# A mixture of experts as one stream of weight pieces in a hand-written order, and leading tiles in five pools

## The chip, the core and the metric

The kernel runs on one core of a Trainium2 chip. TensorE (PE) multiplies; its weight loads, which bring the stationary operand, are listed apart as PEld. VectorE is DVE, ScalarE is ACT, GpSimd is POOL; SP issues most of the DMAs. SBUF and PSUM are the on-chip memories, HBM holds weights and inputs. The metric is the device time of one execution in microseconds (us); the median of three runs is given.

## What is computed

A transformer of three layers on 256 tokens of width 1024: sliding-window attention and a dense feed-forward block, block-sparse attention and a mixture of experts, then a block of a linear and an axial attention, attention over a memory, and a second feed-forward block. All inputs are float32. The change is in the mixture of experts:

```python
def _swiglu(x, w_gate, w_up, w_down):
    return (jax.nn.silu(x @ w_gate) * (x @ w_up)) @ w_down

def _moe(x, router, w_gate, w_up, w_down):
    ...
    vals, ids = lax.top_k(logits, TOP_K)            # TOP_K = 2
    w = jax.nn.softmax(vals, axis=-1)
    gate = jnp.sum(jax.nn.one_hot(ids, N_EXPERTS, dtype=jnp.float32) * w[..., None], axis=1)
    for e in range(N_EXPERTS):                      # 8 experts, D_FF = 3584
        out = out + gate[:, e:e + 1] * _swiglu(xt, w_gate[e], w_up[e], w_down[e])
```

## The kernel before

**A product.** To keep float32 accuracy with the fast matmul, each operand is split into a high and a low part, and a product is three matmuls: high by high, high by low, low by high (lines 274, 275, 276). In `gemm` the activations are stationary, 128 by 128, and the weights move, 512 columns at a time.

**A piece of weights** is 2 by 128 rows by 512 columns, 512 KB. `fetch` (line 210) has SP issue its DMA into one of `NRAW = 9` raw buffers; `split_w` casts it on ACT into `wh` (line 256) and subtracts on DVE for `wl` (line 257), into one of `NSPL = 5` split buffers. A raw buffer is free again when DVE has read it, a split buffer when PE has used it. Where `fine` is set, the split is made in halves (lines 253, 254).

**The experts' loop** (`moe`) goes over pairs of experts. A one-hot matrix `oh` of the pair gathers its tokens by matmul (`bring`, line 1102) into `xg`, high and low, in four steps of two slices; each step is called when the first gate product reaches its slices. Then for each expert, seven times: a gate product of four pieces, Silu on ACT into `sil` (line 1162), an up product of four pieces, the multiplication on DVE (line 1170), four transposes of the result (line 186) and their split into `h` by ACT and DVE (lines 189, 190). After these come two down products of 14 pieces each; each is scaled into `yh` and `yl` (lines 1179, 1180), scattered back to the token order by four matmuls (lines 1084, 1085) and added (line 1087). The last 16 slices of the last expert's second down product are loaded early into four parked tiles (`park`). Five pieces are split and nine fetched ahead of the loop.

**The order.** All these are written one after the other, and the tile scheduler decides at build time how they follow each other on each engine; on the chip each engine runs its list in order, and each instruction waits for what it needs. PSUM has four `mm` buffers, two `tr` and two `at`.

**Pools.** Tiles stand one behind the other in their pool, so a small tile at its head moves those behind it. The pool "moe" opens with such a tile of 48 floats per partition. The pools "heads" (`oh`, `ol`, twice), "ffn" (`hh`, `hl`, used by both feed-forward blocks), "mixm" (`mh`, `ml`, `ah`, `al`) and "mem" (another `oh`, `ol`, on the right side) have none; these tiles are the stationary operands of the products behind them.

Of the kernel before, what the change touches and what calls it, by code (L numbers as in the profile page):

```python
# [8 lines left out]
F32 = mybir.dt.float32  # L9
# [7 lines left out]
P = 128  # L17
D = 1024
# [6 lines left out]
def f(ap):  # L25
    return ap.bitcast(F32)
# [72 lines left out]
class Net:  # L99
# [417 lines left out]
    def swa(self):  # L517
        nc, A, tc = self.nc, self.A, self.tc
        self.fine = True
        with ExitStack() as c0:  # L520
            po = c0.enter_context(self.pool("heads", 1))
            oh = po.tile([P, 8, T], F32R, name="oh")
            ol = po.tile([P, 8, T], F32R, name="ol")
            c = c0.enter_context(ExitStack())
# [88 lines left out]
    def ffn_body(self, Wg, g0, Wu, u0, dff, Wd, emit, scale=None, beside=lambda p: None):  # L613
# [3 lines left out]
        chunks = [(j, min(512, dff - j)) for j in range(0, dff, 512)]  # L617
        with ExitStack() as c:
            p = c.enter_context(self.pool("ffn", 1))
            hh = p.tile([P, nkf, T], F32R, name="hh")  # L620
            hl = p.tile([P, nkf, T], F32R, name="hl")
            sil = {}

            def emit_g(i, c0, n, ps, tts=(0, 1)):
                for tt in tts:
                    s = p.tile([P, 512], F32, tag="sil", name="sil", bufs=3)
                    nc.scalar.activation(s[:, :n], ps[tt][:, :n], AF.Silu, scale=scale[tt] if scale else 1.0)
                    sil[tt] = s

            j, n = chunks[0]  # L630
            self.gemm(self.xs, Wg, KD, [(g0 + j, n)], emit_g, apart=(0,))

            def emit_u(i, c0, n, ps, tts=(0, 1)):
                for tt in tts:
                    s = sil[tt][:, :n]
                    nc.vector.tensor_mul(s, s, ps[tt][:, :n])
                    self.transpose_split(s, n // P, hh[:, :n // P, tt * P:(tt + 1) * P], hl[:, :n // P, tt * P:(tt + 1) * P])

            self.gemm(self.xs, Wu, KD, [(u0 + j, n)], emit_u)
            R = None  # L640
            if scale:

                ones, R = (p.tile([P, w], F32, name=x) for x, w in (("ones", P), ("R", T)))
                nc.gpsimd.memset(ones, 1.0)
                tp = self.tr.tile([P, T], F32, tag="tr", name="tr")
                for tt in range(2):
                    nc.gpsimd.tensor_scalar_mul(R[:, tt * P:(tt + 1) * P], self.idn, scale[tt])
                    nc.tensor.matmul(tp[:, tt * P:(tt + 1) * P], ones, R[:, tt * P:(tt + 1) * P], start=True, stop=True)
                nc.scalar.copy(R, tp)

            for j, n in chunks[1:]:
                s = p.tile([P, 4, T], F32, tag="silT", name="sil", bufs=2)
                k0 = j // P

                def gate(b, ps):
                    x = s[:, 2 * b:2 * b + 2]
                    if R is not None:
                        nc.vector.tensor_mul(x, ps, R.unsqueeze(1).to_broadcast([P, 2, T]))
                    nc.scalar.activation(x, x if R is not None else ps, AF.Silu)

                def up(b, ps):
                    x, k = s[:, 2 * b:2 * b + 2], k0 + 2 * b
                    nc.vector.tensor_mul(x, x, ps)
                    nc.scalar.copy(hh[:, k:k + 2], x)
                    nc.vector.tensor_sub(hl[:, k:k + 2], x, f(hh[:, k:k + 2]))

                self.gemm_f(Wg, g0 + j, n, gate)
                self.gemm_f(Wu, u0 + j, n, up)
                if j == 512:
                    beside(p)  # L670
            self.gain = None
            self.gemm(lambda k, tt: (hh[:, k, tt * P:(tt + 1) * P], hl[:, k, tt * P:(tt + 1) * P]), Wd, nkf,
                      [(0, 512), (512, 512)], emit, apart=(1,))
# [29 lines left out]
    def nsa(self):  # L703
        nc, A, tc = self.nc, self.A, self.tc
        self.fine = True
        with ExitStack() as c0:
            po = c0.enter_context(self.pool("heads", 1))
            c = c0.enter_context(ExitStack())
            p = c.enter_context(self.pool("nsa", 1))
            qT = tuple(p.tile([P, 8, T], F32R, name=f"q{n}") for n in "hl")  # L710
# [272 lines left out]
    def moe(self):  # L983
# [5 lines left out]
        with ExitStack() as c0:  # L989
# [103 lines left out]
            def gather(oh):  # L1093

                xg = [p.tile([P, KD, 2, P], F32R, tag=f"xg{n}", name="xg") for n in "hl"]

                def bring(k0):
                    for X, x in zip((Xh, Xl), xg):
                        ps = self.mm.tile([P, 2, 2, P], F32, tag="mm", name="mm")
                        for k in range(2):  # L1100
                            for tt in range(2):
                                nc.tensor.matmul(ps[:, k].rearrange("p a s -> p (a s)"), X[tt][:, (k0 + k) * P:(k0 + k + 1) * P],  # L1102
                                                 oh[:, tt].rearrange("p a s -> p (a s)"), start=tt == 0, stop=tt == 1)
                        if X is Xl:
                            nc.scalar.copy(x[:, k0:k0 + 2], ps)  # L1105
                        else:
                            nc.vector.tensor_copy(x[:, k0:k0 + 2], ps)

                there = set()

                def xs(i, k):
                    if k not in there:
                        there.update((k, k + 1))
                        bring(k)
                    return xg[0][:, k, i], xg[1][:, k, i]

                return xs


            for n in range(NRAW + NSPL):  # L1120
# [22 lines left out]
                    nc.vector.scalar_tensor_tensor(y, ps if h else y, mu, out["g"][:, cs], op0=OP.subtract, op1=OP.mult)  # L1143
                    nc.vector.scalar_tensor_tensor(x, y, rs, out["b"][:, cs], op0=OP.mult, op1=OP.add)

            for e0 in range(0, NE, 2):
                oh, back = onehots((e0, e0 + 1), 0)
                brought = gather(oh)
                if e0 == 0:

                    last = [self.xp.tile([P, 4, 512], F32, tag="xh", name="parked"), *(p.tile([P, 4, 512], F32, name=f"parked{n}") for n in range(3))]
                    for n, t in enumerate(last):
                        self.park(Wd[NE - 1], (NF - 16 + n * 4) * P, 512, t)
                for i in range(2):
                    e = e0 + i
                    hs = {}
                    xs = lambda k, tt: brought(i, k)
                    st = {}

                    def emit_g(_, c0, n, ps, tts=(0, 1)):  # L1160
                        st["s"] = p2.tile([P, 512], F32, tag="sil", name="sil")
                        nc.scalar.activation(st["s"], ps[0], AF.Silu)

                    for j in range(F // 512):
                        self.gemm(xs, Wg[e], KD, [(j * 512, 512)], emit_g, tts=(0,))
                        if i == 0 and j == 0:
                            oT, gs = back()

                        def emit_u(_, c0, n, ps, tts=(0, 1)):
                            nc.vector.tensor_mul(st["s"], st["s"], ps[0])  # L1170
                            hs[j] = [p.tile([P, 4, P], F32R, tag=f"h{n}", name="h", bufs=7) for n in "hl"]
                            self.transpose_split(st["s"], 4, hs[j][0], hs[j][1])

                        self.gemm(xs, Wu[e], KD, [(j * 512, 512)], emit_u, tts=(0,))

                    def emit_d(_, c0, n, ps, tts=(0, 1)):
                        yh = p.tile([P, 512], F32R, tag="yh", name="yh")
                        yl = p.tile([P, 512], F32R, tag="yl", name="yl")
                        nc.scalar.mul(yh, ps[0], gs[:, i:i + 1])
                        nc.vector.scalar_tensor_tensor(yl, ps[0], gs[:, i:i + 1], f(yh), op0=OP.mult, op1=OP.subtract)  # L1180
                        scatter(yh, yl, oT, i, c0, e == NE - 1)

                    if e == NE - 1:
                        out["g"] = self.bcast(A["ln_gain"][1, 1], D, "gb", pool=p, tag="xgh")
                        out["b"] = self.bcast(A["ln_bias"][1, 1], D, "bb", pool=p, tag="xgl")
                    for c0 in (0, 512):
                        self.fine = e == NE - 1 and c0 > 0
                        self.gemm(lambda k, tt: (hs[k // 4][0][:, k % 4], hs[k // 4][1][:, k % 4]), Wd[e], NF,
                                  [(c0, 512)], emit_d, tts=(0,))

        self.routes.close()

# [134 lines left out]
    def mixer(self):  # L1327
# [3 lines left out]
        with ExitStack() as c0:  # L1331
# [46 lines left out]
            with self.tc.high_priority(offset=-1000):  # L1378
                self.memory_kv()
            pm = c0.enter_context(self.pool("mixm", 1))  # L1380
            mh = pm.tile([P, KD, T], F32R, name="mh")
            ml = pm.tile([P, KD, T], F32R, name="ml")
            ah = pm.tile([P, 8, T], F32R, name="ah")
# [461 lines left out]
    def memory(self):  # L1845
# [3 lines left out]
        with ExitStack() as c0:  # L1849
# [3 lines left out]
            qT = p.tile([P, 8, T], F32, name="qT")  # L1853
            oh = po.tile([P, 8, T], F32R, tag="oh", name="oh")
            ol = po.tile([P, 8, T], F32R, tag="ol", name="ol")
            ms = lambda k, tt: (oh[:, k, tt * P:(tt + 1) * P], ol[:, k, tt * P:(tt + 1) * P])
            self.new_xT()
            with self.pool("pre", 1) as px:
# [212 lines left out]
```

## Time and profile before

| | |
|---|---|
| median of three runs | 2371.4 us (2369.98 to 2378.29) |
| the profiled execution | 2368.1 us; its span 2366.3 us |
| busy, share of the span | PE 96%, PEld 81%, DVE 75%, ACT 61%, POOL 3% |
| mean granted clock of TensorE | 0.977 |
| HBM read | 536 MB, 228 GB/s over the span |

Busy shares are means over stages that differ. A matmul is listed from its start to the modelled end of its pipeline, so two that follow each other overlap; the rate is read from start to start. "Idle before" is the time in which the engine stood still ahead of an instruction, with what ended it.

### The profile page before, as it was taken

To read this page: it belongs to the slowest core of one execution; us is meant where nothing else is said; L and a number is where in the kernel's file an instruction comes from. 1 tells how busy PE (TensorE), PEld (TensorE's weight loads), DVE (VectorE), ACT (ScalarE), POOL (GpSimd) and SP (SyncE) were. 2 spreads that over 40 slices of the span, in tenths; PEclk is the share of its full clock that TensorE was granted. 3 is DMA by queue.
4 is the path that set the end of the run, shared out by engine and by line. 5 is a ranking of instruction groups with operands and counts; after the bars stand their busy time and mean duration, and the time that the engine had idled before them with its cause. 6 is when DMAs were issued, how large, how long until landed. Compare 5 with 4: busy or idle time off the path is not lost.

```text
span 2366.3 us, 35741 instructions
## 1 busy us (share of the span) xinstructions
PE 2261.2 (96%) x12969; PEld 1923.0 (81%) x12969; DVE 1778.9 (75%) x2849; ACT 1440.7 (61%) x2386; POOL 66.1 (3%) x78
## 2 busy tenths in 40 slices
PE   8999998999899999999999999996898999989998
PEld 6699977887787787778777877775898888988997
DVE  7765559766788988889888888887857765666664
ACT  5664436665677767777777777774553554455553
POOL 0000000000000000000000000001110110000000
PEclk9999999999899999999999999998998999999999
DMA  8366555434899999999999999994333213543761
GB/s 242 98 198 192 187 160 175 148 107 145 289 364 350 350 350 345 357 352 343 346 365 349 358 334 357 355 323 132 108 90 99 74 54 110 170 143 137 260 200 46
DMA packets 319711, 541.96 MB, mean 229 GB/s; under 512 B 21839, under 2 KB 95015, under 8 KB 319271
## 3 DMA queue, kind: packets, MB, share of 16 engines
q1 hardware_dynamic: 309680, 528.93, 66.6%
q10 hardware_dynamic: 9847, 10.67, 1.5%
q8 instruction: 104, 1.70, 0.3%
q14 instruction: 80, 0.66, 0.1%
HBM read 536.38 MB, written 3.15 MB: 228 GB/s over the span
## 4 chain that ended last, share of the span: by engine, by line
PE 65%; DVE 4%; issue 3%; ACT 1%; POOL 1%; DMA 0%; DVEq 0%; POOLq 0%; ACTq 0%
PE mm L275 15%; PE mm L276 15%; PE mm L274 15%; PE tr L186 2%; PE mm L688 1%; PE mm L318 1%; PE mm L689 1%; PE mm L687 1%; PE mm L319 1%; PE mm L317 1%; PE tr L1701 1%; DVE wl L254 1%; PE at L1712 1%; PE at L1715 1%; PE mm L1102 1%
## 5 line engine op out<-in xcount | busy, mean ns | idle before, releaser
L257 DVE TENSOR_TENSOR wl<-w,wh 128x1024 fp32r<-128x1024 f32 x755 | 884.4, 1219 | 171.9 <-ACT wh L256 166.9
L256 ACT CAST wh<-w 128x1024 fp32r<-128x1024 f32 x755 | 753.9, 1050 | 179.3 <-PE mm L276 114.2
L275 PE MATMUL mm<-wl,xg 128*128 128x512 f32 x896 | 364.8, 407 | 0.6
L276 PE MATMUL mm<-wh,xg 128*128 128x512 f32 x896 | 351.4, 392 | 0.0
L274 PE MATMUL mm<-wh,xg 128*128 128x512 f32 x896 | 349.7, 392 | 0.0
L253 ACT CAST wh<-w 128x512 fp32r<-128x512 f32 (+1 forms) x378 | 216.3, 616 | 135.5 <-PE mm L276 59.6
L254 DVE TENSOR_TENSOR wl<-w,wh 128x512 fp32r<-128x512 f32 (+1 forms) x378 | 247.1, 682 | 52.0 <-ACT wh L253 51.5
L275 PEld LDWEIGHTS mm<-wl,xg 128*128 128x128 f32 x896 | 168.4, 188 | 65.8 <-DVE wl L257 35.7
L274 PEld LDWEIGHTS mm<-wh,xg 128*128 128x128 f32 x896 | 168.2, 188 | 36.0
L276 PEld LDWEIGHTS mm<-wh,xg 128*128 128x128 f32 x896 | 168.8, 188 | 30.9 <-ACT xg L1105 1.4
L687 PE MATMUL mm<-xh,wh 128*128 128x256 f32 x672 | 187.4, 279 | 0.0
L689 PE MATMUL mm<-xl,wh 128*128 128x256 f32 x672 | 187.3, 279 | 0.0
L688 PE MATMUL mm<-xh,wl 128*128 128x256 f32 x672 | 187.3, 279 | 0.0
L275 PE MATMUL mm<-wl,h 128*128 128x512 f32 x448 | 177.1, 395 | 1.7 <-DVE wl L257 1.7
L276 PE MATMUL mm<-wh,h 128*128 128x512 f32 x448 | 174.6, 390 | 0.0
L274 PE MATMUL mm<-wh,h 128*128 128x512 f32 x448 | 174.5, 390 | 0.0
L687 PEld LDWEIGHTS mm<-xh,wh 128*128 128x128 f32 x672 | 127.4, 190 | 0.0
L688 PEld LDWEIGHTS mm<-xh,wl 128*128 128x128 f32 x672 | 126.3, 188 | 0.0
L689 PEld LDWEIGHTS mm<-xl,wh 128*128 128x128 f32 x672 | 126.2, 188 | 0.0
L275 PEld LDWEIGHTS mm<-wl,h 128*128 128x128 f32 x448 | 84.1, 188 | 22.8 <-DVE wl L257 6.1
L274 PEld LDWEIGHTS mm<-wh,h 128*128 128x128 f32 x448 | 84.1, 188 | 18.0 <-ACT wh L256 0.2
L276 PEld LDWEIGHTS mm<-wh,h 128*128 128x128 f32 x448 | 84.2, 188 | 16.6 <-issue 0.2
(615 smaller groups left out, 4466.7 us busy)
## 6 DMA issues: line engine op xcount, KB each, us to landing
w<-in_moe_w_gate_dram SPq DMA_DIRECT2D x224, 512.0 KB, 5.6
w<-in_moe_w_up_dram SPq DMA_DIRECT2D x224, 512.0 KB, 5.5
w<-in_moe_w_down_dram SPq DMA_DIRECT2D x216, 512.0 KB, 5.9
w<-in_w_in_dram SPq DMA_DIRECT2D x60, 512.0 KB, 3.8
w<-in_w_ffn_in_dram SPq DMA_DIRECT2D x40, 512.0 KB, 9.8
w<-in_ffn_w_gate_dram SPq DMA_DIRECT2D x28, 512.0 KB, 4.5
w<-in_ffn_w_up_dram SPq DMA_DIRECT2D x28, 512.0 KB, 4.4
w<-in_ffn_w_down_dram SPq DMA_DIRECT2D x28, 512.0 KB, 3.6
```

Source lines behind the costliest of these rows:

```text
L186: nc.tensor.transpose(ps[:, k, :], src[:, (k0 + k) * P:(k0 + k + 1) * P], self.idn)
L253: nc.scalar.copy(wh[:, ks, :n], w[:, ks, :n])
L254: nc.vector.tensor_sub(wl[:, ks, :n], w[:, ks, :n], f(wh[:, ks, :n]))
L256: nc.scalar.copy(wh[:, :nk, :n], w[:, :nk, :n])
L257: nc.vector.tensor_sub(wl[:, :nk, :n], w[:, :nk, :n], f(wh[:, :nk, :n]))
L274: nc.tensor.matmul(o, h, wh[:, k, :sn], start=k0 + k == 0, stop=False)
L275: nc.tensor.matmul(o, h, wl[:, k, :sn], start=False, stop=False)
L276: nc.tensor.matmul(o, l, wh[:, k, :sn], start=False, stop=k0 + k == nk - 1)
L317: nc.tensor.matmul(o, h, wh[:, k, :n], start=k0 + k == 0, stop=False)
L687: nc.tensor.matmul(o, wh[:, k, js], h, start=first and j % 2 == 0, stop=False)
L688: nc.tensor.matmul(o, wl[:, k, js], h, start=False, stop=False)
L689: nc.tensor.matmul(o, wh[:, k, js], l, start=False, stop=last and j % 2 == 1)
```

## The change

The experts' loop is written anew. All pieces of all experts are one list; `weights()` keeps five of them split and hands out the next. `product` runs a product piece by piece and, after each piece, what has been put off for that place. `put_off(n, first, then)` places the PE part of a step n pieces later and its copies one piece after that; it is used for the transposes (`hidden`), the scatter (`spread_out`) and the gather of the next pair, which now goes into the first down product of a pair's second expert. From behind the first gather to the last down product, `manual_schedule` makes the order on PE, ACT and DVE that of the text. SP and POOL are left to the scheduler. Five pools get a small tile at the head, or behind `oh` and `ol` in "mem".

```diff
             po = c0.enter_context(self.pool("heads", 1))
+            po.tile([P, 16], F32, name="lead")
...
             p = c.enter_context(self.pool("ffn", 1))
+            p.tile([P, 16], F32, name="lead")
...
             po = c0.enter_context(self.pool("heads", 1))
+            po.tile([P, 16], F32, name="lead")
...
                 def bring(k0):
...
+                    def first():
+                        ps = [self.mm.tile([P, 2, 2, P], F32, tag="mm", name="mm") for _ in range(2)]
+                        for X, o in zip((Xh, Xl), ps):
...
+                        return ps
+                    def then(ps):
+                        nc.vector.tensor_copy(xg[0][:, k0:k0 + 2], ps[0])
+                        nc.scalar.copy(xg[1][:, k0:k0 + 2], ps[1])
+                    return first, then
+                return xg, bring
...
-            for e0 in range(0, NE, 2):
+            pieces = []
+            for e in range(NE):
+                for j in range(0, F, 512):
+                    pieces += [(W[e], k * P, j, False) for W in (Wg, Wu) for k in range(0, KD, 2)]
+                pieces += [(Wd[e], k * P, c, e == NE - 1 and c > 0) for c in (0, 512) for k in range(0, NF, 2)]
+            pieces, held, later = iter(pieces), [], []
+            def weights():
+                while len(held) < NSPL:
+                    q = next(pieces, None)
+                    if q is None:
+                        break
+                    held.append(self.load_w(q[0], q[1], 2, q[2], 512, fine=q[3]))
+                return held.pop(0)
+            def product(nk, x):
+                ps = self.mm.tile([P, 512], F32, tag="mm", name="mm")
+                for k0 in range(0, nk, 2):
+                    wh, wl = weights()
+                    for k in range(2):
+                        h, l = x(k0 + k)
+                        nc.tensor.matmul(ps, h, wh[:, k], start=k0 + k == 0, stop=False)
+                        nc.tensor.matmul(ps, h, wl[:, k], start=False, stop=False)
+                        nc.tensor.matmul(ps, l, wh[:, k], start=False, stop=k0 + k == nk - 1)
+                    now = [w for w in later if w[0] == 1]
+                    later[:] = [[n - 1, w] for n, w in later if n > 1]
+                    for _, w in now:
+                        w()
+                return ps
+            def put_off(n, first, then):
+                got = []
+                later.append([n, lambda: got.append(first())])
+                later.append([n + 1, lambda: then(got[0])])
+            def pair(e0):
                 oh, back = onehots((e0, e0 + 1), 0)
-                brought = gather(oh)
...
-                                  [(c0, 512)], emit_d, tts=(0,))
+                xg, bring = gather(oh)
+                for n, k0 in enumerate(range(0, KD, 2)):
+                    if e0:
+                        put_off(n + 1, *bring(k0))
+                    else:
+                        w = lambda a=bring(k0): a[1](a[0]())
+                        w() if n < 2 else later.append([n - 1, w])
+                return back, xg
+            def hidden(s, t):
...
+                put_off(2, first, then)
+            def spread_out(yh, yl, oT, i, c0, stats):
...
+                put_off(2, first, then)
+            nxt = pair(0)
...
+            order = c0.enter_context(ExitStack())
+            order.enter_context(tc.manual_schedule(engines={mybir.EngineType.PE, mybir.EngineType.Activation, mybir.EngineType.DVE}))
+            for e in range(NE):
+                i = e % 2
+                if i == 0:
+                    back, xg = nxt
+                x = lambda k: (xg[0][:, k, i], xg[1][:, k, i])
+                hs = []
+                for j in range(F // 512):
+                    ps = product(KD, x)
+                    if i == 0 and j == 0:
+                        oT, gs = back()
+                    t = p2.tile([P, 512], F32, tag="sil", name="sil")
+                    nc.scalar.activation(t, ps, AF.Silu)
+                    ps = product(KD, x)
+                    nc.vector.tensor_mul(t, t, ps)
+                    hs.append([p.tile([P, 4, P], F32R, tag=f"h{n}", name="h", bufs=7) for n in "hl"])
+                    hidden(t, hs[j])
+                if e == NE - 1:
+                    out["g"] = self.bcast(A["ln_gain"][1, 1], D, "gb", pool=p, tag="xgh")
+                    out["b"] = self.bcast(A["ln_bias"][1, 1], D, "bb", pool=p, tag="xgl")
+                for c in (0, 512):
+                    if i and c == 0 and e < NE - 1:
+                        nxt = pair(e + 1)
+                    if e == NE - 1 and c:
+                        order.close()
+                    ps = product(NF, lambda k: (hs[k // 4][0][:, k % 4], hs[k // 4][1][:, k % 4]))
+                    yh = p.tile([P, 512], F32R, tag="yh", name="yh")
+                    yl = p.tile([P, 512], F32R, tag="yl", name="yl")
+                    nc.scalar.mul(yh, ps, gs[:, i:i + 1])
+                    nc.vector.scalar_tensor_tensor(yl, ps, gs[:, i:i + 1], f(yh), op0=OP.mult, op1=OP.subtract)
+                    if e == NE - 1 and c:
+                        scatter(yh, yl, oT, i, c, True)
+                    else:
+                        spread_out(yh, yl, oT, i, c, e == NE - 1)
...
             pm = c0.enter_context(self.pool("mixm", 1))
+            pm.tile([P, 32], F32, name="lead")
...
             oh = po.tile([P, 8, T], F32R, tag="oh", name="oh")
             ol = po.tile([P, 8, T], F32R, tag="ol", name="ol")
+            po.tile([P, 48], F32, name="tail")
```

`bring`'s matmuls, `hidden`'s transposes and splits and `spread_out`'s matmuls and additions are those of before, cut in two.

## Rows read from the trace of the kernel before

**Rows 1.** Stretches of the loop: us, busy by engine (x count), PEclk, DMA share, GB/s

```profile
604.00:620.00 16.00, 16.00 (x80) 13.68 (x79) 7.77 (x13) 8.49 (x11) 0.00 (x0) 0.89 0.69 228
...
640.00:660.00 20.00, 20.00 (x93) 16.46 (x93) 19.15 (x20) 16.26 (x18) 0.00 (x0) 1.00 1.05 387
...
1200.00:1300.00 100.00, 99.60 (x435) 77.90 (x434) 87.89 (x84) 71.44 (x80) 0.00 (x0) 1.00 1.00 357
...
600.00:1612.00 1012.00, 1007.14 (x4497) 799.12 (x4497) 884.55 (x875) 736.04 (x827) 0.00 (x0) 1.00 0.97 343
```

**Rows 2.** What SP's own queue waited for, 620 to 1600: us, times, longest

```profile
SPq L210 <- DVE wl L257: 661.5, 639, 6.1
```

**Rows 3.** Waits of the engines in the loop: us, times, longest

```profile
PEld mm L275 <- DVE wl L257: 41.8, 134, 1.1
...
PEld tr L186 <- DVE sil L1170: 13.2, 45, 0.3
```

**Rows 4.** ACT in order of time: start, us, what, idle before it

```profile
968.89 1.06 ACT L256 CAST wh<-w 128x1024 fp32r<-128x1024 f32 x1 [0.30 <-PE mm L276]
...
970.25 1.06 ACT L256 CAST wh<-w 128x1024 fp32r<-128x1024 f32 x1 [0.30 <-PE mm L276]
...
999.91 0.60 ACT L1162 ACTIVATE sil<-mm 128x512 f32<-128x512 f32 x1 [1.34 <-PE mm L276]
...
1000.41 4.84 ACT L256 CAST wh<-w 128x1024 fp32r<-128x1024 f32 x5
...
1007.06 0.59 ACT L189 CAST h<-tr 128x512 fp32r<-128x512 f32 x1 [1.81 <-PE tr L186]
...
1047.52 0.60 ACT L1162 ACTIVATE sil<-mm 128x512 f32<-128x512 f32 x1 [1.34 <-PE mm L276]
```

**Rows 5.** PE in order of time, in a down product

```profile
975.03 0.39 PE L275 MATMUL mm<-wl,h 128*128 128x512 f32 x1
...
976.39 0.39 PE L275 MATMUL mm<-wl,h 128*128 128x512 f32 x1
```

**Rows 6.** PE's weight loads in order of time, in gate and up products

```profile
1002.76 0.19 PEld L275 LDWEIGHTS mm<-wl,xg 128*128 128x128 f32 x1 [0.36 <-DVE wl L257]
...
1006.37 0.42 PEld L186 LDWEIGHTS tr<-idn,sil 128*128 128x128 f32 x4 [0.30 <-DVE sil L1170]
```

**Rows 7.** DVE in order of time, in gate and up products

```profile
1001.48 3.50 DVE L257 TENSOR_TENSOR wl<-w,wh 128x1024 fp32r<-128x1024 f32 x3 [0.82 <-ACT wh L256]
...
1005.63 0.69 DVE L1170 TENSOR_TENSOR sil<-sil,mm 128x512 f32<-128x512 f32 x1 [0.65 <-PE mm L276]
...
1008.50 0.68 DVE L190 TENSOR_TENSOR h<-tr,h 128x512 fp32r<-128x512 f32 x1
```

**Rows 8.** Line 275: times, first and last start us, by tile

```profile
L275 PEld LDWEIGHTS mm<-wl,xg x896: 186/188/333, 604.5 to 1567.9; 128*128 128x128 f32 x180
...
L275 PE MATMUL mm<-wl,h x448: 387/389/793, 689.3 to 1610.6; 128*128 128x512 f32 x150
```

**Rows 9.** Stretches with matmuls of 256 columns: `mh`, `xh`, the memory's `oh`

```profile
2072.00:2094.00 22.00, 22.00 (x188) 21.83 (x187) 13.19 (x23) 10.61 (x23) 0.16 (x1) 1.00 0.61 191
...
2108.00:2126.00 18.00, 18.00 (x161) 18.00 (x160) 8.12 (x13) 8.38 (x16) 0.00 (x0) 1.00 0.48 146
...
2147.00:2170.00 23.00, 23.00 (x193) 22.98 (x192) 9.52 (x17) 8.25 (x17) 0.55 (x1) 1.00 0.00 1
```

**Rows 10.** Groups of instructions, 620 to 1600: busy us, mean ns, idle before

```profile
L257 DVE TENSOR_TENSOR wl<-w,wh 128x1024 fp32r<-128x1024 f32 x650 | 755.8, 1218 | 52.0 <-ACT wh L256 50.7 <-DMA w<-in_moe_w_down_dram 0.3
```

**Rows 11.** Line 210, the fetches: duration ns, first and last start us

```profile
L210 SPq DMA_DIRECT2D w<-in_moe_w_gate_dram x215: 367/368/747, 620.7 to 1547.9; - x108
```

**Rows 12.** DMA issues, 636 to 662 us: count, KB each, median us to landing

```profile
w<-in_moe_w_up_dram SPq DMA_DIRECT2D x11, 512.0 KB, 7.0
```

**Rows 13.** PE in order of time, the first block's down product

```profile
274.70 0.40 PE L275 MATMUL mm<-wl,hh 128*128 128x512 f32 x1
...
276.80 0.40 PE L275 MATMUL mm<-wl,hh 128*128 128x512 f32 x1
```

More of the change, by code (lines that the diff above doesn't have):

```diff
@@ L1097, in bring @@
                 def bring(k0):
[L1098 to L1117, printed above, removed]
+                    def first():
+                        ps = [self.mm.tile([P, 2, 2, P], F32, tag="mm", name="mm") for _ in range(2)]
+                        for X, o in zip((Xh, Xl), ps):
+                            for k in range(2):
+                                for tt in range(2):
+                                    nc.tensor.matmul(o[:, k].rearrange("p a s -> p (a s)"), X[tt][:, (k0 + k) * P:(k0 + k + 1) * P],
+                                                     oh[:, tt].rearrange("p a s -> p (a s)"), start=tt == 0, stop=tt == 1)
+                        return ps
[4 more added lines that the diff above has]
+                return xg, bring
             for n in range(NRAW + NSPL):
@@ L1144, in done @@
                     nc.vector.scalar_tensor_tensor(x, y, rs, out["b"][:, cs], op0=OP.mult, op1=OP.add)
-            for e0 in range(0, NE, 2):
-                oh, back = onehots((e0, e0 + 1), 0)
-                brought = gather(oh)
[L1149 to L1188, printed above, removed]
-                                  [(c0, 512)], emit_d, tts=(0,))
@@ new lines, in product @@
+            def product(nk, x):
+                ps = self.mm.tile([P, 512], F32, tag="mm", name="mm")
+                for k0 in range(0, nk, 2):
+                    wh, wl = weights()
+                    for k in range(2):
+                        h, l = x(k0 + k)
[7 more added lines that the diff above has]
+                return ps
@@ new lines, in hidden, with first, then @@
+            def hidden(s, t):
+                def first():
+                    ps = self.tr.tile([P, 4, P], F32, tag="tr", name="tr")
+                    for k in range(4):
+                        nc.tensor.transpose(ps[:, k], s[:, k * P:(k + 1) * P], self.idn)
+                    return ps
+                def then(ps):
+                    nc.scalar.copy(t[0], ps)
+                    nc.vector.tensor_sub(t[1], ps, f(t[0]))
+                put_off(2, first, then)
+            def spread_out(yh, yl, oT, i, c0, stats):
+                def first():
+                    ps = [self.at.tile([P, 512], F32, tag="at", name="at") for _ in range(2)]
+                    for tt in range(2):
+                        nc.tensor.matmul(ps[tt], oT[:, i, tt], yh, start=True, stop=False)
+                        nc.tensor.matmul(ps[tt], oT[:, i, tt], yl, start=False, stop=True)
+                    return ps
+                def then(ps):
+                    for tt in range(2):
+                        y = acc[tt][:, c0:c0 + 512]
+                        nc.vector.tensor_add(y, y, ps[tt])
+                        if stats:
+                            nc.vector.bn_stats(self.st[tt][:, 0], y)
+                put_off(2, first, then)
@@ new lines, in moe @@
+            nxt = pair(0)
+            last = [self.xp.tile([P, 4, 512], F32, tag="xh", name="parked"), *(p.tile([P, 4, 512], F32, name=f"parked{n}") for n in range(3))]
+            for n, t in enumerate(last):
+                self.park(Wd[NE - 1], (NF - 16 + n * 4) * P, 512, t)
+            order = c0.enter_context(ExitStack())
[33 more added lines that the diff above has]
+                        spread_out(yh, yl, oT, i, c, e == NE - 1)
```

## The prediction

> **What bounds the kernel now.** I read the page's slices first: the slices in which DMA stands at nine tenths or more, 600 to 1610 us, are the experts' loop, and it is 43% of the span, so what the change is worth is read there. The table of stretches comes second. Over 600 to 1612 PE is busy 1007 of 1012 us, DVE 885, ACT 736, and DMA moves 343 GB/s at a share of 0.97 [rows 1]. Three resources look full, so the question is which one waits for which. The wait list and SP's own answer that. SP waits 661.5 us for DVE to free raw buffers [rows 2], so DMA is asked for no more than the splitting frees, and DMA is not the bound. PE waits for DVE: 41.8 us before the matmul that needs `wl`, 13.2 us before the transposes that need `sil` [rows 3]. A PE that is "100% busy" thus hides stalls, because a matmul counts as busy beyond the start of the next one.
>
> The timelines say why. In the down products ACT casts one piece every 1.36 us with 0.30 us of waiting for PE [rows 4]: six matmuls at (976.39 - 975.03)/6 = 0.2267 us are 1.36 us [rows 5], so PE sets the pace there and nothing is lost. In the gate and up products a period (one gate and one up product of 512 columns, eight pieces) takes (1047.52 - 999.91)/4 = 11.90 us [rows 4]. PE has 48 x 0.2267 = 10.88 us of matmuls and 0.42 us of transposes [rows 5, 6] to do in it, 11.30 us. The missing 0.60 us starts on ACT: it stands at `sil` for 1.34 us until the gate product ends [rows 4], while a split buffer for the next piece is already free; the casts behind it then run back to back, DVE starts 0.82 us late [rows 7], and PE waits 0.36 us for `wl`, then 0.30 us for the product that it is to transpose [rows 6].
>
> **The pool of lost time.** The loop runs from 604.5 (first gate weight load) to 1610.6 (last down matmul) [rows 8]: 1006.1 us. PE's own work in it: 8 x 504 = 4032 matmuls x 0.2267 = 914.1; 56 groups of transposes x 0.42 = 23.5; scatters of 15 half products, 60 x 0.2267 = 13.6; gathers, three pairs of 32 matmuls of 256 columns and half of the first pair's, 112 x 0.117 (the 188 matmuls in 22.0 us of another 256-column stretch [rows 9]) = 13.1; the one-hot transposes and gate sums of four pairs, an estimate of 12 x 0.105 = 1.3 each, 5.2. Together 969.5. The clock stands at 0.89 over 604 to 620 [rows 1], at the lower level for part of it, about 2 us. Lost: 1006.1 - 971.5 = 34.6 us. The other way, 56 periods x 0.60 = 33.6. The two agree, so nearly all the loss lies in the gate and up products.
>
> **Part 1, the stream.** `weights()` holds five pieces, so the split of piece p+4 is traced ahead of piece p's matmuls and, in the hand order, stands on ACT and DVE ahead of the `sil` or the product that waits for piece p's end. Count from the end of piece p. The buffer of p+4 is free when p-1 ends, 1.36 us earlier; the cast takes 1.06 [rows 4], the subtraction 1.22 [rows 10], so `wl` is there 0.9 us after the end of p, and PE wants it three pieces, 4.1 us, after. `sil` delays the next cast by 0.6 us, the product the next subtraction by 0.69 [rows 4, 7]; both fit into that 3.2 us. Per period ACT has 8 x 1.0 + 0.6 + 0.59 = 9.2 us and DVE 8 x 1.17 + 0.69 + 0.68 = 10.7 us (3.50 us for three, back to back [rows 7]) beside PE's 11.30, so each can catch up. The stall named above has no cause left; what is late next is PE itself.
>
> **Part 2, the put-offs.** Transposes, copies, scatters and gathers stay the same in number. The transposes move two pieces back, 2.72 us after the product ends, its multiplication is done after about 1.7 us, so PE arrives 1.0 us behind it. On PE everything behind a transpose that waits would wait too, on ACT and DVE the splits behind its copies. There are 56 + 15 + 12 = 83 such points. Each may cost nothing or, if buffers in PSUM come late for the second half of a gather, some tenths of a microsecond. I take 0.05 each, 4 us, with 0 and 0.4 (33 us, the whole pool) as ends; nearer to 0, since the down products already run in just this manner at 1.36 us. A cast that waits for its landing would now hold up `sil` behind it, but it is SP that waits for the splitting [rows 2], not the reverse. The gather's DVE and ACT copies go from the head of a pair into a down product, whose DVE is idle 1.36 - 1.17 = 0.19 us a piece, 2.7 us in 14 pieces, enough for four copies of 0.6. The two broadcast loads at the last expert keep their place and queue; the order of SP's fetches stays that of the pieces. Below nothing the cost can't go beyond the pool: gain 34.6 - 4 = **30 us**, ends 2 and 35.
>
> **DMA must keep up.** From 620.7 [rows 11] 658 pieces of 0.524 MB, 345 MB, must land; with PE at its pace the loop ends near 1578, the last nine pieces (eight of them parked early) take 12 us, so 345 MB in 945 us: 365 GB/s, 372 in a gate and up period and 385 in a down product. Over 640 to 660, after a pause, it held 387 GB/s [rows 1] with 7.0 us to landing [rows 12], and nine buffers give a fetch some 9.9 us. It is enough, with 2% to spare in the down products. [...]
>
> **Part 3, the leading tiles.** They shift `hh`, `oh`, `ah`, `mh` and their low parts by 64 to 192 bytes per partition. Where `hh` is stationary, 512 columns take (276.80 - 274.70)/9 = 0.2333 us, against 0.2267 for `h` in the experts' pool, which opens with a leading tile already [rows 5, 13]. 256 columns take 0.117 with `mh`, 0.119 with the memory's `oh` (23.0/193), and 0.112 (18.0/161) where `xh` moves [rows 9]. PE is busy throughout in these stretches, so spacing is time. If all reach the better figure: 600 with `hh` x 6.6 ns = 4.0; 384 of `ah` and `mh` x 5 ns = 1.9; 192 of `oh` x 7 ns = 1.3; 192 in the two attentions, about 0.5: 7.7 us. Nothing in the trace says which shift gives which spacing, so the other end is that they move the wrong way by half as much, +4. I take **4 us** gain, nearer to the full sum since one shifted pool in the trace has the good spacing. [...]
>
> **The sum.** The profiled execution took 2368.1 us, its span is 2366.3. 2368.1 - 30 - 4 = 2334. The median of the three runs lies 3.3 us above the profiled one, so **2337 us**.
>
> **Rivals.** (a) *DMA ceiling.* If no more can be kept up than the best 100 us show, 357 GB/s [rows 1], 345 MB take 966 us from 620.7, and with 12 us at the end the loop ends at 1599 instead of 1611: 2371 - 12 - 4 = 2355. For it: the share is 1.00 there; against: 387 GB/s, and SP's waits. (b) *DVE becomes the bound.* In order behind ACT, each subtraction takes 1.22 us alone and not 1.17, and if each also waits 0.1 us for its cast, a period takes 8 x 1.32 + 1.37 = 11.9, no gain; half of that, 11.6, gives 17 us: 2350. (c) *Slower: PE queues behind late products.* The place is the transposes and scatters, 71 of them. PE in hand order can't run the next matmuls first, as the scheduler's order let it. The margin is 1.0 us; with DVE 1.5 us late at each the pool of 34.6 is eaten up, that is the point from which it decides; 2.0 us late costs 71 x 1.0 - 34.6 = 36: 2371 + 36 - 4 = 2403. For it: DVE has the least slack, 5%; against: while PE waits DVE catches up. (d) *The tiles do nothing*: 2371 - 30 = 2341. For it: no row shows a tile shifted and not shifted; against: the two spacings of one shape. [...] (e) *The order doesn't change*, or ACT waits elsewhere for the same: 2371 - 4 = 2367.
>
> **How the numbers follow.** Chances: the forecast 0.54 (2327 to 2346), (a) 0.10, (b) 0.15, (c) 0.06, (d) 0.08, (e) 0.07. The range 2326 to 2358 takes in the forecast, (a), (b) and (d), 0.87, less their own spread. A measurement tells about 0.5% from no change, 12 us, so faster means below 2359.5: forecast, (b), (d) and most of (a), 0.85; within 0.5% (e) and the rest of (a), 0.10; slower (c), less what of it is small, 0.05.
>
> **What would show it.** Right: in the loop no `sil` wait on ACT followed by a row of casts back to back, but casts at 1.36 us with `sil` between; periods of 11.3 to 11.4 us; the 41.8 and 13.2 us under 5 each; DMA at 360 to 370 GB/s; `hh` at 0.227. Wrong: PE waits at transposes (c), casts that wait for landings at under 360 GB/s (a), DVE without a gap at 11.6 us (b).

## The result, and the profile after

The changed kernel takes **2339.06 us** (median of four runs, 2336.1 to 2343.94) beside 2374.85 us for the kernel before (four runs too; the table above has the first three): a ratio of 0.985, 95% interval 0.982 to 0.988. Predicted were 2337 us, range 2326 to 2358. Measured once more it took 2341.93 beside 2370.59, 0.988 (0.984 to 0.992).

The profiled executions are 2368.1 us before and 2343.9 after, spans 2366.3 and 2342.1. The one before is faster than all four runs of its median, the one after is the slowest of its four, so the profiles show 24 us where the medians show 36. Where those 24 us lie is read best from the first and last instructions of the loop, the line group that answers to [rows 8]; the low-part matmul is now line 1170:

```profile
L1170 PEld LDWEIGHTS mm<-wl,xg x896: 187/188/330, 604.2 to 1542.1; 128*128 128x128 f32 x180
...
L1170 PE MATMUL mm<-wl,h x448: 387/389/799, 687.0 to 1583.5; 128*128 128x512 f32 x150
```

The loop runs from 604.2 to 1583.5, 979.3 us, where it took 1006.1: **26.8 us** less. The products with `hh` give 2.6 more and the later products with a shifted tile 0.7 (both below); the second feed-forward block's gate and up products lose 3.7, which is not the change's doing (below too). Another 1.8 us go between the first block's down product, which ends 2.1 us earlier, and the loop, which begins only 0.3 us earlier; the granted clock over 360 to 400 us is 0.87 there, where it was 0.96. Together these are 24.6 us, within 0.4 of the difference.

ACT in order of time in gate and up products, start, duration, what, idle before it; it answers to [rows 4]:

```profile
978.33 0.60 ACT L1245 ACTIVATE sil<-mm 128x512 f32<-128x512 f32 x1 [0.30 <-PE mm L1171]
...
1012.43 0.60 ACT L1245 ACTIVATE sil<-mm 128x512 f32<-128x512 f32 x1 [0.32 <-PE mm L1171]
...
1023.78 0.60 ACT L1245 ACTIVATE sil<-mm 128x512 f32<-128x512 f32 x1 [0.30 <-PE mm L1171]
```

`sil` waits 0.30 us, no longer 1.34, and the period is (1023.78 - 978.33)/4 = 11.36 us instead of 11.90. The wait list of the loop (604 to 1600; us, times, longest) answers to [rows 3]:

```profile
ACT wh L256 <- PE mm L1171: 166.5, 489, 1.2
...
ACT sil L1245 <- PE mm L1171: 17.2, 55, 0.4
...
PEld mm L1106 <- DVE oh L1060: 4.6, 6, 1.2
```

PE's 41.8 us for `wl` and 13.2 us for `sil` are gone from it. ACT now waits 166.5 us for PE to free split buffers, so PE leads; before it was 36.0 us:

```profile
ACT wh L256 <- PE mm L276: 36.0, 118, 0.5
```

One wait of PE is new, 4.6 us for the one-hots `oh`. The stretches, columns as in [rows 1], and SP's own wait, as in [rows 2]:

```profile
1200.00:1300.00 100.00, 99.16 (x448) 81.58 (x447) 93.77 (x93) 79.97 (x85) 0.00 (x0) 1.00 1.02 370
600.00:1600.00 1000.00, 984.18 (x4508) 814.76 (x4508) 917.19 (x901) 777.04 (x842) 3.44 (x5) 0.99 0.97 349
```

```profile
SPq L210 <- DVE wl L257: 637.1, 640, 2.3
```

In the same 100 us DMA moves 370 GB/s where it moved 357, DVE is busy 93.8 where it was 87.9, and SP still waits for the splitting, not for DMA.

### The profile page after: what moved, and what is told of

The parts are those of the page before. It is cut to its first block, busy times and chain, and to the rows that moved or that the text cites. A ratio compares the mean times of both kernels' runs of the same rounds, so it can differ in the third digit from the quotient of the medians.

```text
span 2342.1 us, 35734 instructions
## 1 busy us (share of the span) xinstructions
PE 2235.6 (95%) x12969; PEld 1939.6 (83%) x12969; DVE 1798.7 (77%) x2849; ACT 1475.2 (63%) x2386; POOL 66.5 (3%) x78
## 4 chain that ended last, share of the span: by engine, by line
PE 65%; DVE 4%; issue 3%; ACT 1%; POOL 1%; DMA 0%; DVEq 0%; POOLq 0%; ACTq 0%
PE mm L1169 13%; PE mm L1171 13%; PE mm L1170 13%; PE mm L274 2%; PE mm L276 2%; PE mm L275 2%; PE mm L690 1%; PE mm L689 1%; PE mm L691 1%; PE mm L318 1%; PE mm L319 1%; PE mm L317 1%; PE tr L1201 1%; DVE wl L254 1%; PE tr L1779 1%
## 5 line engine op out<-in xcount | busy, mean ns | idle before, releaser
L257 DVE TENSOR_TENSOR wl<-w,wh 128x1024 fp32r<-128x1024 f32 x755 | 905.8, 1222 | 186.1 <-ACT wh L256 156.1
L256 ACT CAST wh<-w 128x1024 fp32r<-128x1024 f32 x755 | 788.1, 1053 | 302.6 <-PE mm L1171 166.5
L1170 PE MATMUL mm<-wl,xg 128*128 128x512 f32 x896 | 349.0, 389 | 0.0
```

What stands on the lines that cost most here:

```text
L256: nc.scalar.copy(wh[:, :nk, :n], w[:, :nk, :n])
L257: nc.vector.tensor_sub(wl[:, :nk, :n], w[:, :nk, :n], f(wh[:, :nk, :n]))
L1170: nc.tensor.matmul(ps, h, wl[:, k], start=False, stop=False)
```

## The experiments

Loop is the time from the first weight load of a gate product's low part to the last such matmul of a down product, as above (in the last kernel, which has no low part, of the high part).

| kernel | median us | ratio to before (95%) | loop us |
|---|---|---|---|
| before | 2370 to 2375 | 1 | 1006.1 |
| the change | 2339.06 | 0.985 (0.982 to 0.988) | 979.3 |
| the change, again | 2341.93 | 0.988 (0.984 to 0.992) | 979.6 |
| loop alone | 2350.9 | 0.991 (0.988 to 0.994) | 979.4 |
| leading tiles alone | 2370.84 | 1.0005 (0.998 to 1.003) | 1005.4 |
| one-hots earlier | 2337.15 | 0.985 (0.981 to 0.989) | 975.1 |
| three pieces held | 2352.47 | 0.991 (0.987 to 0.994) | 991.5 |
| two pieces held | 2492.54 | 1.050 (1.046 to 1.055) | 1120.6 |
| transposes one piece late | 2364.6 | 0.996 (0.993 to 0.999) | 1002.3 |
| lead of 32 in the experts' pool | 2349.18 | 0.990 (0.987 to 0.993) | 988.0 |
| low part of the weights left out | 2279.93 | 0.962 (0.956 to 0.969) | 908.2 |

Single runs of one kernel differ by some 8 to 30 us where there are four or more (loop alone: 2337.7 to 2367.2 in 12 runs), while the loop's length in the profile comes back within 0.3 us in the three profiles with the same loop (979.3, 979.6, 979.4). So the loop's length decides below, wherever a kernel changes the loop.

### The two parts apart

The change again, with nothing edited:

> The whole change once more, beside the three runs below. Theory (the experts' loop is worth about 27 us, the five leading tiles about 0 to 4, and some 4 us come and go between executions): a ratio to the kernel before of 0.983 to 0.988, a loop of 979 to 981 us where the profile of the kernel before has 1006, and the second feed-forward block within 1 us of the kernel before this time, since its code is the same. Rival (the leading tile in the feed-forward pool makes that block slower): the block is again 3 to 4 us longer than before.

The new loop without the leading tiles:

```diff
-            po.tile([P, 16], F32, name="lead")
-            p.tile([P, 16], F32, name="lead")
...
-            po.tile([P, 48], F32, name="tail")
```

> The new experts' loop without the five leading tiles. Theory A (the tiles bring the 4 us of the prediction): 4 us, 0.17%, over the whole change, so a ratio to before of about 0.987 where the whole change has 0.985. Theory B (the tiles bring about nothing, gains at some products being lost at others): within 1.5 us of the whole change. Both expect the loop itself at 979 to 981 us.

The kernel before with the five leading tiles:

```diff
+            po.tile([P, 16], F32, name="lead")
+            p.tile([P, 16], F32, name="lead")
...
+            po.tile([P, 48], F32, name="tail")
```

> The kernel before with the five leading tiles alone. Theory A: 4 us faster than the kernel before, ratio 0.9983 (ends 0.9967 and 1.0017). Theory B: 1.000. In the profile, by both, the products with hh as stationary operand go from 0.233 to 0.227 us; by B something else takes as much back, first of all the 256-column gate and up products of the feed-forward blocks. The experts' loop stays at 1006 us.

The loop's gain is there without the tiles (979.4), and not there with the tiles alone (1005.4). For the tiles the medians can't decide: the tiles alone give 1.0005 with an interval that holds 0.9983 too, and the loop alone is 9 us over the whole change with intervals that meet. The profile can. The two feed-forward blocks' down products, line 275 with `hh`, count, durations, first and last start; first the loop alone, then the whole change, then (first block) the tiles alone:

```profile
L275 PE MATMUL mm<-wl,hh x112: 392/397/398, 285.3 to 364.5; 128*128 128x512 f32 x112
...
L275 PE MATMUL mm<-wl,hh x88: 393/394/395, 2297.9 to 2357.7; 128*128 128x512 f32 x88
```

```profile
L275 PE MATMUL mm<-wl,hh x112: 387/389/397, 274.0 to 351.1; 128*128 128x512 f32 x112
...
L275 PE MATMUL mm<-wl,hh x88: 389/389/397, 2275.2 to 2334.4; 128*128 128x512 f32 x88
```

```profile
L275 PE MATMUL mm<-wl,hh x112: 387/389/395, 279.9 to 357.1; 128*128 128x512 f32 x112
```

The first stretch takes 79.2 us without the tile, 77.1 and 77.2 with it, and the matmuls are listed at 389 instead of 397 ns. In the second block 59.8 become 59.2. That is 2.1 + 0.6 = 2.7 us, and **2.6 us** against the kernel before (79.2 and 59.7), where the prediction's sum had 4.0 for `hh`. All nine profiles with the tile have 77.1 or 77.2 and 59.1 or 59.2 us, the two without it 79.2 and 59.7 or 59.8. The products with `ah`, `mh` and the memory's `oh` have 256 columns, and those differ between profiles of the same code. The feed-forward blocks show it: 256-column gate and up products, second block, in the kernel before, the change, the change again, and the loop alone (line 688 in the first and the last):

```profile
L688 PE MATMUL mm<-xh,wl x288: 276/276/367, 2199.5 to 2298.4; 128*128 128x256 f32 x144
```

```profile
L690 PE MATMUL mm<-xh,wl x288: 276/281/366, 2172.1 to 2274.7; 128*128 128x256 f32 x144
```

```profile
L690 PE MATMUL mm<-xh,wl x288: 276/276/369, 2173.2 to 2272.0; 128*128 128x256 f32 x144
```

```profile
L688 PE MATMUL mm<-xh,wl x288: 276/281/367, 2194.8 to 2297.4; 128*128 128x256 f32 x144
```

102.6 us and 98.8 us are the same kernel, built and run twice, and 102.6 is there without a tile as well. So the 3.7 us that the change's profile loses here are not the tile's, and the rival of the first expectation, a slower block by the tile, falls.

For the other three tiles the same reading of the low-part line, first to last start, gives small gains. With `ah` it is 24.2 us in both profiles without the tiles and 23.7 to 24.0 in the nine with them; with `mh` 22.9, and 22.1 to 22.9; with the memory's `oh` 22.6, and 21.4 to 22.3. In the change's profile that is 0.3 + 0 + 0.4 = 0.7 us, in others up to 2.5, where the prediction's sum had 1.9 + 1.3. With two profiles without tiles, and 256-column products that differ by themselves, the size is not settled.

### The wait that was not foreseen: one-hots

The change makes the next pair's one-hots where its gather begins. The timeline of the change there, all engines (start, duration, what, idle before it):

```profile
1052.82 0.68 DVE L1247 TENSOR_TENSOR sil<-sil,mm 128x512 f32<-128x512 f32 x1
1053.42 1.11 DVE L1060 TENSOR_SCALAR oh<-slots,pos,sel 128x128 fp32r<-128x128 f32 x4
1054.07 0.19 PEld L1106 LDWEIGHTS mm<-oh,Xh 128*128 128x128 f32 x1 [1.22 <-DVE oh L1060]
...
1054.58 0.42 PEld L1106 LDWEIGHTS mm<-oh,Xh 128*128 128x128 f32 x3 [0.33 <-DVE oh L1060]
```

DVE finishes the last product and starts at 1053.4 on four one-hots; PE's gather stands one piece behind the end of that product and waits 1.22 + 0.33 = 1.55 us, three times in the loop. The experiment makes them a gate and up period earlier:

```diff
+                    if i and j == F // 512 - 1 and e < NE - 1:
+                        made = onehots((e + 1, e + 2), 0)
                     ps = product(KD, x)
...
-                        nxt = pair(e + 1)
+                        nxt = pair(e + 1, made)
```

> The changed kernel, with the one-hots of the next pair made one gate and up period earlier, ahead of the last gate product of a pair's second expert, rather than at the first down product. Theory (the gather's matmuls wait on PE for the one-hots, which in the text's order stand on DVE behind splits and the last product of the gate and up part; that is some 1.5 us for each of three pairs): 4.6 us, 0.2%, under the whole change, the first down product of such an expert 43.2 instead of 44.75 us, and no wait of line 1106 for the one-hots in the profile. Rival (what is late there is the two mm buffers that the gather wants at once, or the DVE as a whole, and the wait only changes its name): within 1 us of the whole change.

```profile
L1170 PEld LDWEIGHTS mm<-wl,xg x896: 187/188/330, 612.6 to 1546.2; 128*128 128x128 f32 x180
...
L1170 PE MATMUL mm<-wl,h x448: 387/389/799, 695.6 to 1587.7; 128*128 128x512 f32 x150
```

The loop takes 975.1 us, 4.2 less than in the change (4.6 expected), and the wait is off the list, so it did not only change its name. The medians, 2337.15 and 2341.93 for the change from runs on the same chip, are as far apart, but single runs of either differ by more; the loop is the evidence. It is the shortest loop of the kernels that do the whole computation.

### Does the lookahead do it? Three and two pieces held

The lookahead is the number of pieces that `weights()` keeps split ahead of PE, five in the change. Here it is three:

```diff
-                while len(held) < NSPL:
+                while len(held) < 3:
```

> The changed kernel with three pieces held split instead of five, so that only the split of piece p+2 stands ahead of what waits for piece p. Theory (the lookahead ahead of sil removes the stall, and its length matters): behind sil the cast of p+3 ends 0.3 + 0.6 + 1.06 = 2.0 us after the end of p and its subtraction at 3.2; PE wants wl 2 x 1.36 + 0.23 = 2.95 us after the end of p. So 0.2 to 0.3 us is lost in each of 56 periods, 14 us (0 to 25): a loop of about 993 us, a period of 11.6, the wait of PE's weight loads for wl back with some 10 us. Rival (the put-offs and the hand order give the gain, the lookahead gives nothing): the loop stays at 980.

ACT in the same stretch with three held, and its wait list:

```profile
1003.31 0.60 ACT L1245 ACTIVATE sil<-mm 128x512 f32<-128x512 f32 x1 [1.23 <-PE mm L1171]
...
1049.78 0.60 ACT L1245 ACTIVATE sil<-mm 128x512 f32<-128x512 f32 x1 [1.23 <-PE mm L1171]
```

```profile
ACT sil L1245 <- PE mm L1171: 72.1, 55, 1.9
...
PEld mm L1170 <- DVE wl L257: 19.0, 53, 0.4
```

`sil` waits 1.23 us again, PE waits for `wl` again 53 times (19.0 us in all, where some 10 were expected), the period is (1049.78 - 1003.31)/4 = 11.62, and the loop 991.5: the theory's 11.6 and 993. But these are 12.2 of the 26.8 us only, though `sil` waits nearly as long as before the change (1.34). What doesn't come back is PE's wait for the transposes, 13.2 us before [rows 3]: they are still put off, and the list has none.

Here it is two:

```diff
-                while len(held) < NSPL:
+                while len(held) < 2:
```

> The changed kernel with two pieces held split: only the split of p+1 stands ahead of what waits for p. Theory: wl of p+2 comes 3.2 us after the end of p where PE wants it 1.6 us after, 1.6 us lost behind sil and up to 0.6 behind the product on DVE, 56 times: 90 to 125 us, a loop of 1070 to 1105 us, slower than the kernel before (1006), though transposes, scatters and gathers are put off as in the whole change. Rival (the put-offs give the gain): the loop stays between 980 and 1006 us.

```profile
PEld mm L1170 <- DVE wl L257: 117.7, 160, 1.1
...
ACT yh L1261 <- PE mm L1171: 61.4, 14, 4.4
...
PEld mm L1169 <- ACT wh L256: 35.0, 61, 0.8
```

The loop takes 1120.6 us, 114 more than before, with every put-off of the change in place. The theory's direction holds and the rival falls; its upper end was 16 us short of the measured size. PE also waits for the cast itself (35.0 us), which the theory had not counted; how much of the 16 us that is, the run doesn't show.

### The margin of the transposes

The transposes of a product come one piece behind it instead of two:

```diff
-                put_off(2, first, then)
+                put_off(1, first, then)
```

> The changed kernel with the transposes put off by one piece instead of two. Theory (the multiplication on DVE is done some 1.7 us after the product's end, and PE in hand order can't go past a transpose that waits): PE comes 1.36 us after the product's end and waits 0.35 us, 56 times: 20 us, a loop of 1000 us, 2359 in all, and a wait of the transposes for sil of about 20 us in the profile. Rival (DVE catches up because the splits ahead are done early, or the wait is taken up by PE's queue): under 5 us.

```profile
PEld tr L1201 <- DVE sil L1247: 39.6, 56, 0.7
...
PE tr L1201 <- DVE sil L1247: 16.0, 56, 0.3
```

PE waits at all 56 groups (the weight load and the matmul behind it wait for the same thing, so the two rows are not to be added), where in the change it waits at none. The period on ACT:

```profile
1002.68 0.60 ACT L1245 ACTIVATE sil<-mm 128x512 f32<-128x512 f32 x1 [0.30 <-PE mm L1171]
...
1038.24 0.60 ACT L1245 ACTIVATE sil<-mm 128x512 f32<-128x512 f32 x1 [0.30 <-PE mm L1171]
```

It is (1038.24 - 1002.68)/3 = 11.85 us, 0.49 more than in the change, 27 us for 56 groups. The loop is only 23.0 us longer (20 expected), and 3.6 us of the rest are the wait for the one-hots, which falls from 4.6 to 1.0 us. In the change DVE ends a product's multiplication at 1018.74 + 0.68 = 1019.42, and PE begins its transposes at 1020.39, 0.97 us later:

```profile
1018.74 0.68 DVE L1247 TENSOR_TENSOR sil<-sil,mm 128x512 f32<-128x512 f32 x1
```

So two pieces leave 0.97 us, and one piece, 1.36 us less, is too short. This is rival (c) of the prediction made real: PE in hand order does stand behind a late product, and only the second piece keeps it from doing so. With five pieces held the loop is still 1002.3, 3.8 us under the kernel before; so the gain needs both, the split ahead and the transposes two pieces late. No run leaves the new text to the scheduler's order, so what the hand order does by itself is not shown.

### Where the stationary operand stands

The experts' pool opens with a smaller tile, so all behind it stand 64 bytes per partition earlier:

```diff
-            p.tile([P, 48], F32, name="lead")
+            p.tile([P, 32], F32, name="lead")
```

> The changed kernel with the leading tile of the experts' pool cut from 48 to 32 floats, so that xg and h, the stationary operands of the experts' loop, stand 64 bytes per partition earlier. Theory (the spacing of matmuls depends on where the stationary operand stands against the moving one, as hh shows with 0.233 and 0.227 us): 4032 matmuls of 512 columns at 0.229 to 0.2327 instead of 0.2267 us, 8 to 24 us, taken at 14: a loop of 994 us. Rival (hh's gain has another cause than the place): the loop stays at 980 us. [...]

PE in a down product with the lead of 32:

```profile
960.03 0.39 PE L1170 MATMUL mm<-wl,h 128*128 128x512 f32 x1
...
966.21 0.39 PE L1170 MATMUL mm<-wl,h 128*128 128x512 f32 x1
```

27 matmuls in 6.18 us, 0.2289 us each, where [rows 5] have 0.2267, and a loop of 988.0, 8.7 us longer: the low end of what was expected. The rival of no change falls. Why the place matters, the runs don't show.

### Was DMA close to a limit?

All of the weights' low part is left out in the experts' loop, the subtraction on DVE and one matmul in three, so the time is not that of the same computation:

```diff
+        if self.only_high:
+            self.nc.scalar.copy(wh[:, :nk, :n], w[:, :nk, :n])
+            return wh, None
...
-                        nc.tensor.matmul(ps, h, wl[:, k], start=False, stop=False)
```

> The changed kernel with the low part of the weights left out in the experts' loop: DVE subtracts nothing there and PE has two matmuls per slice instead of three, so that DMA is the only thing asked for the same as before. Per period PE needs 32 x 0.2267 + 0.42 = 7.7 us, ACT 8 x 1.06 + 1.2 = 9.7, and 4.19 MB have to land. Rival (a) of the prediction, a ceiling of 357 GB/s: a period of 11.7 us, 345 MB in 966 us, a loop of about 991 us, no shorter than the whole change's 980 in spite of a third less work on PE. Theory (387 GB/s can be kept up): a period of 10.8 us, 345 MB in 891 us, a loop of about 914 us, 2275 in all. Between: a ceiling of 372 GB/s gives 11.3 us, just PE's own period, and would mean that the whole change stands at DMA's limit as well.

A stretch of the loop, columns as in [rows 1], and ACT:

```profile
800.00:900.00 100.00, 90.30 (x357) 61.40 (x356) 12.86 (x20) 83.11 (x90) 0.00 (x0) 0.98 1.05 387
...
620.00:1500.00 880.00, 777.61 (x2999) 512.05 (x2998) 119.10 (x183) 729.72 (x784) 0.00 (x0) 0.98 1.05 385
```

```profile
966.50 1.05 ACT L240 CAST wh<-w 128x1024 fp32r<-128x1024 f32 x1 [0.31 <-DMA w<-in_moe_w_up_dram]
967.85 1.05 ACT L240 CAST wh<-w 128x1024 fp32r<-128x1024 f32 x1 [0.30 <-DMA w<-in_moe_w_up_dram]
```

Now the casts wait for landings, one piece every 1.35 us, and DMA moves 385 GB/s over 880 us. The loop takes 908.2 us (theory 914, rival 991). Rival (a) falls: the 357 GB/s of before were what was asked for, not what could be had.

## Why the prediction was right, point by point

**The stall and its removal: right, and shown.** Rival (e), an order that stays the same, falls with the first row of ACT after. The period went from 11.90 to 11.36 us, predicted 11.3 to 11.4: 56 x 0.54 = 30 us of the 34.6 in the pool. That the split's place ahead of `sil` is needed follows from the two kernels with fewer pieces held: the wait for `wl` comes back as the lookahead shrinks, with the put-offs kept. It is not the whole: with the lookahead kept and the transposes put off by one piece, the loop is back at 1002.3 us. The prediction's count of 0.9 us for `wl` against 4.1 us wanted says that five is ample; three are 0.2 short by the same count, and cost 12.2 us (56 x 0.22).

**The put-offs: the size near, the place wrong.** I charged 0.05 us at each of 83 points, 4 us, and named as the risk late PSUM buffers in a gather. What was lost is 4.6 us at three points, on DVE: I counted the gather's copies into the down product's slack, but not the four one-hots (1.11 us) that its step issues ahead of them, which in text order stand behind the last product. At the transposes, where I gave a margin of 1.0 us, there is no wait, and the margin measures 0.97. The 979.3 us are 8 above PE's own 971.5 of the prediction: 4.6 at the one-hots and 56 x 0.06 in the periods (11.36 against 11.30), for which the profile names no wait. The 0.06 lie at the transposes, which I had at 0.42 us from the list of their weight loads [rows 6]. On PE the second matmul behind a group starts 0.67 us after the group (1009.02 to 1009.69), 0.44 more than one matmul's 0.23, and the next six take 1.40 us instead of 1.36. So the gain of the loop was put at 30 us and came out at 26.8.

**DMA: right.** 370 GB/s in the stretch that showed 357, SP still waiting for DVE, and 385 GB/s kept up when asked. Against the down products' 385 there is no room at all, though: 1.35 us a landing and 1.36 us a piece on PE. The 385 GB/s of the run without the low part decide against rival (a) for this kernel on one core.

**DVE: not the bound, but near.** Rival (b) had 11.6 us a period; it came out at 11.36. Four subtractions take 4.83 us, 1.21 each and not the 1.17 of [rows 7], so DVE has 8 x 1.21 + 0.69 + 0.68 = 11.0 us of work in 11.36:

```profile
1014.00 4.83 DVE L257 TENSOR_TENSOR wl<-w,wh 128x1024 fp32r<-128x1024 f32 x4 [0.63 <-ACT wh L256]
```

**The leading tiles: sign right, size near, the parts wrong.** 4 us were taken, about half of the full sum of 7.7. The profile of the change shows 2.6 at `hh` and 0.7 at `ah`, `mh` and the memory's `oh`, and the last three differ between profiles by more than that. What the tiles give in the two attentions (0.5 in the sum) was not read. The term of `hh` alone was put at 4.0 by 600 x 6.6 ns. The first block gave its share, 2.1 us; the second gave 0.6 for its 264 matmuls, because without the tile its spacing is 59.8/261 = 0.229 us, not 0.2333 (88 starts of line 275 with two other matmuls between them are 261 steps): I had read the first block only [rows 13] and taken it for both. Rival (d), no effect at all, falls with the 79.2 and 77.1 us.

**The total.** The 2337 us came out within 2.1 of the median, which is better than its parts and in part luck. The loop gave 26.8 us where 30 stood and the tiles about 3.3 where 4 stood, 30 us together instead of 34; the first medians lie 36 us apart, the second ones 29. The median's place above the profiled run (3.3 us taken) is itself uncertain by more than these differences.

## What to carry to other kernels

When an engine runs its list in order, an instruction that waits for the end of a product holds up all splitting behind it (in the kernel before ACT stood 1.34 us at `sil`, then cast five pieces without a gap [rows 4]); count from the end of that product how many pieces must be split ahead so that the next one is there when PE wants it, and put the rest of the work (transposes, copies) as many pieces later as its inputs take, plus a margin. Count everything that a moved step issues, on every engine: here it was four small instructions on the busiest helper that were left out. Where executions scatter by more than an effect, compare the length of the one stage in the profile, not the whole time.

## What was not expected of the hardware

**The same code at two spacings.** The 256-column gate and up products of the second feed-forward block take 102.6 us in one profile and 98.8 in another of the same kernel (above). The first block has two lengths as well, 138.1 and 134.3, and the kernel before has the longer in its first block and the shorter in its second (98.9). The 512-column products with `hh` keep their spacing over all profiles and change with the tile. What sets the spacing of the 256-column ones, and whether it goes with the build or with the execution, the runs don't show, since each profile is of a build of its own.

**The clock falls in some executions and not in others, with the same work before it.** Stretches of the change, first in its first profile, then in the one taken again:

```profile
40.00:60.00 20.00, 19.31 (x102) 14.11 (x100) 14.98 (x42) 11.89 (x40) 0.00 (x0) 1.00 0.61 172
60.00:80.00 20.00, 20.00 (x108) 14.10 (x107) 15.44 (x50) 16.64 (x63) 0.00 (x0) 1.00 0.19 53
```

```profile
40.00:60.00 20.00, 19.31 (x95) 14.13 (x94) 13.90 (x40) 10.65 (x35) 0.00 (x0) 0.91 0.63 174
60.00:80.00 20.00, 20.00 (x59) 12.94 (x59) 10.49 (x29) 9.47 (x37) 0.00 (x0) 0.50 0.18 52
```

PE is busy 19.3 of 20 us in both; then the granted clock is 1.00 in one and 0.50 in the other over the stretch, with 108 and 59 matmuls done. Six of the eleven profiles have this fall. Over the 12 runs of the loop alone the mean granted clock goes with the time: 2337.7 us at 0.977, 2367.2 at 0.967. In the two executions above the experts' loop begins at 604.2 us and at 608.5, ahead of any changed loop code. In the kernel before the clock is 0.50 from 604 to 607.5 us, the lower level for which the prediction takes 2 us there. What decides whether the clock falls, the runs don't show.

**A landing rate that holds.** In the kernel without the low part, 512 KB arrive about every 1.36 us, 385 GB/s, for 880 us on the one core of this program.
